# Stick-breaking attention: stay factors kept and scanned in PSUM, the mask as a matrix product

## The chip, the cores and the metric

One NeuronCore of a Trainium2 chip runs the whole kernel in one launch. The metric is the device time of that launch in microseconds; the core is the only one, so it is also the slowest. PE is the matrix engine, DVE the vector engine, ACT the activation engine, POOL GpSimd, SP the engine whose queue issues the DMAs. [...]

## The reference

One transformer layer on 2048 tokens of width 1024: adaptive layer norm, an input projection, three mixers (gated chunks, stick-breaking attention, dilated-window attention), an output projection, and a feed-forward part with a causal convolution. The change touches the stick-breaking mixer, six heads of width 64:

```python
z = jnp.einsum('bqhd,bkhd->bhqk', q_blk, k).astype(jnp.float32) * scale      # scale = 1/8
log_beta = jax.nn.log_sigmoid(z)
log_stay = jnp.where(before, jax.nn.log_sigmoid(-z), 0.0)                     # before: k_pos < q_pos
tail = lax.cumsum(log_stay, axis=3, reverse=True) - log_stay
weight = jnp.where(before, jnp.exp(log_beta + tail), 0.0)
return jnp.einsum('bhqk,bkhd->bqhd', weight.astype(v.dtype), v)
```

The weight of key k for query q is sigmoid(z) at k times the product of sigmoid(-z) over all keys between k and q. The kernel works with these products directly, without logarithms: it scans the stay factors sigmoid(-z) from the last key to the first with a running product.

## The kernel before

All matrix products are in fp32 precision by splitting each operand into a high and a low part (fp32r) and adding three products. Instructions are put in order on each engine by a planner that simulates the program on a cost model of its own; each engine then runs its own list strictly in that order and waits on semaphores. `ORDER` (L1152) lists the units of work for the two halves of the sequence (c = 0 and 1, 1024 tokens each). `st0` to `st5` are stick-breaking heads, `sx5` is head 5 of the first half done in the second list, and a unit with `~` runs aside: after each key chunk of a stick head a few of its steps are released, by the numbers of `RATE`. In the first half the heads lie among projections (`gmv`, `gm`), rotations (`rot`, `stage`) and loads; in the second half, after `rel` (L1090), the six heads run together with the output projection (`op`, `wo_hi`, `yraw`, `xo`) aside. `free` (L1096) gives the stick's memory back, and the FFN takes it for its weights.

`stick` (L498) treats one head for one half. A group g is 256 queries, two blocks j of 128. For each group it goes over key chunks kc of 512 keys, from the one that holds the diagonal (`diag`, kc = top) down to 0. In the diagonal chunk only `nb` blocks of 128 keys exist, so tiles are 128 to 512 wide. The first half has one or two key chunks per group, the second three or four. For each kc and j:

- PE: scores `z` in a PSUM bank, two products (L527, L528).
- ACT: `stay` = sigmoid(-z/8) into one of three long-lived SBUF tiles of 513 columns whose last column is 1.0 (L532), then `beta` = sigmoid(z/8) into SBUF (L533). The z bank is free after that.
- POOL, diagonal only: two `affine_select` on the last 128 columns, setting `stay` to 1 and `beta` to 0 where key >= query (L536).
- DVE: `tensor_tensor_scan` over `stay` backwards, 513 columns, both operands the same SBUF view, initial value 1.0 or the carry of the chunk before (L540), into a new `excl` tile of 513 columns (four slots). Because it starts in the column of ones, `excl` shifted by one is the exclusive product.
- POOL: `beta` times the shifted `excl` (helper `tt`, L78).
- PE: `nb` transposes into the PSUM tile `tr` (L546). ACT copies it to `wh` (helper `copy`, L70), DVE writes the low part `wl` = tr - wh (L78).

After both j, PE adds the products of `wh` and `wl` with the values into `av` (L557). PSUM has eight banks: up to `rel` three for `gm`, two for `z`, two for `tr`, one for `av`; after `rel` two for `gm`, two for `z`, three for `tr`, one for `av` (L1094, L1147).

The tag `excl` serves a second purpose at the start: `ada_first` (L162), called in four steps, takes its accumulator `ada_acc` and the raw V weights of each step from the same four slots. PE reads each accumulator in `ada_ps` (L177).

Of the kernel before, what the change touches and what calls it, by code (L numbers as in the profile page):

```python
# [5 lines left out]
F32 = mybir.dt.float32  # L6
F32R = mybir.dt.float32r
BF16 = mybir.dt.bfloat16
I32 = mybir.dt.int32
AF = mybir.ActivationFunctionType  # L10
ALU = mybir.AluOpType
# [32 lines left out]
class Kernel:  # L44
# [443 lines left out]


    def stick_const(self):  # L490
        self.stay = []
        for k in range(3):
            t = self.pa.tile([P, 513], F32, name=f"stay{k}")
            self.nc.gpsimd.memset(t, 1.0)
            self.stay.append(t)
        self.stay_i = 0

    def stick(self, h, c):  # L498
        nc = self.nc
# [7 lines left out]
        for g in range(4 * c, 4 * c + 4):  # L507
# [3 lines left out]
                av2 = self.ps.tile([P, 512], F32, name="av", tag="av")  # L511
            qo = (g % 2) * 256
            av = av2[:, qo:qo + 256]
            carry = [None, None]
            top = g // 2
            for kc in range(top, -1, -1):
                wh = self.pa.tile([P, 4, 256], F32R, name="wh", tag="wh")
                wl = self.pa.tile([P, 4, 256], F32R, name="wl", tag="wl")
                nbs = []
                for j in range(2):  # L520
                    diag = kc == top
                    nb = (2 * g + j) % 4 + 1 if diag else 4
                    nbs.append(nb)
                    n, o = nb * P, 512 - nb * P
                    kk = khat[kc // 2][:, (kc % 2) * 512:]
                    z = self.ps.tile([P, 512], F32, name="z", tag="z")
                    nc.tensor.matmul(z[:, :n], q1[:, qo + j * P:qo + (j + 1) * P], kk[:, :n], start=True, stop=False)  # L527
                    nc.tensor.matmul(z[:, :n], q2[:, qo + j * P:qo + (j + 1) * P], kk[:, :n], start=False, stop=True)  # L528
                    s = self.stay[self.stay_i]
                    self.stay_i = (self.stay_i + 1) % len(self.stay)  # L530
                    b = self.pa.tile([P, 512], F32, name="beta", tag="beta")
                    nc.scalar.activation(s[:, o:512], z[:, :n], AF.Sigmoid, scale=-0.125)  # L532
                    nc.scalar.activation(b[:, o:512], z[:, :n], AF.Sigmoid, scale=0.125)  # L533
                    if diag:
                        for t, fill in ((s, 1.0), (b, 0.0)):
                            nc.gpsimd.affine_select(out=t[:, 384:512], in_=t[:, 384:512], pattern=[[-1, P]],  # L536
                                                    compare_op=ALU.is_gt, fill=fill, base=0, channel_multiplier=1)
                    x = self.pa.tile([P, 513], F32, name="excl", tag="excl")
                    sr = s[:, o:513][:, ::-1]
                    nc.vector.tensor_tensor_scan(x[:, o:513][:, ::-1], sr, sr, 1.0 if diag else carry[j],  # L540
                                                 op0=ALU.mult, op1=ALU.bypass)
                    carry[j] = x[:, o:o + 1]
                    self.tt("beta", b[:, o:512], b[:, o:512], x[:, o + 1:513], ALU.mult)
                    tr = self.ps.tile([P, 4, P], F32, name="tr", tag="tr")
                    for e in range(nb):
                        nc.tensor.transpose(tr[:, e, :], b[:, o + e * P:o + (e + 1) * P], self.ident)  # L546
                    js = slice(j * P, (j + 1) * P)
                    self.copy("whi_s", wh[:, :nb, js], tr[:, :nb, :])
                    self.tt("v", wl[:, :nb, js], tr[:, :nb, :], wh[:, :nb, js].bitcast(F32), ALU.subtract)
                ops = [(0, 0, wh)]  # L550
                if nbs[1] > nbs[0]:
                    ops += [(nbs[0], P, wh), (nbs[0], P, wl)]
                for e in range(1, nbs[0]):
                    ops += [(e, 0, wh), (e, 0, wl)]
                ops.append((0, 0, wl))
                for m, (e, q0, w) in enumerate(ops):
                    last = nc.tensor.matmul(av[:, q0:256], vhat[kc // 2][:, (kc % 2) * 4 + e, :], w[:, e, q0:256],  # L557
                                            start=(kc == top and m == 0), stop=(kc == 0 and m == len(ops) - 1))
                yield last.ins, sum(nbs) / 8.0
# [287 lines left out]
    def run(self):  # L847
# [191 lines left out]
        for c, order in enumerate(ORDER):  # L1039
            u = units(c, hT[c])  # L1040
            for token in order.split():
# [48 lines left out]
                elif what == "rel":  # L1090
                    finish()
                    self.p1.release()
                    self.ps.release()
                    self.ps = _Bufs(self.pool("ps2", space=PSUM), {**BUFS, "gm": 2, "tr": 3})  # L1094
                    self.po = _Bufs(self.pool("po"), BUFS)
                elif what == "free":  # L1096
                    finish()
# [46 lines left out]

ENGINES = {"whi0": "a", "wlo0": "pppv", "lnt0": "a", "hlo0": "pppv", "lnt": "va", "lnx00": "avv", "lnx01": "aav", "lnx10": "v", "lnx11": "v", "lnx": "va", "hlo": "pvv", "whi": "v", "wlo": "pvv", "qkhi": "avv", "qklo": "v", "cqk": "a", "rot1": "ppv", "rot2": "pv", "rot3": "v", "rothi": "aav", "rotlo": "pvv", "sgu1": "pv", "sgu2": "p", "sguhi": "ap", "sgulo": "ppv", "ya": "aaav", "fold": "a", "beta": "p", "whi_s": "a", "whi_d": "avv", "wom": "v", "wohi": "aav", "wolo": "pv", "ysc": "pv", "yhi": "av", "ylo": "pv", "wuhi": "v", "wulo": "pvv", "wdm": "p", "wdhi": "av", "wdlo": "ppv", "upc": "av", "gv": "pppv", "ghi": "ap", "glo": "ppv", "vhi": "av", "vlo": "v", "uc": "v"}

BUFS = {"gm": 3, "z": 2, "tr": 2, "av": 1, "wraw": 2, "whi": 3, "wlo": 3, "s8": 3, "cs": 2, "tmp2": 2, "khat": 3, "vhat": 2, "q": 2, "beta": 4, "excl": 4, "wh": 2, "wl": 2, "fold": 1, "ys": 1, "x4": 2, "yraw": 2, "ysc": 4, "yh": 2, "yl": 2, "xo": 3, "wuraw": 4, "wul": 3, "wuh": 3, "wdraw": 2, "fx": 2, "up": 3, "dn": 5, "wdh": 2, "wdl": 2, "upc": 3, "cv": 3, "gh": 4, "gl": 4, "fs": 4, "fry": 2, "frr": 2}  # L1147

WOUT = 6
EARLY = (0, 1, 5, 6, 7)  # L1150
# [39 lines left out]
```

## Time and profile before

| what | value |
|---|---|
| median of 3 runs | 2831.44 us (2830.4 to 2834.19) |
| the profiled execution's own time | 2831.72 us |
| its span in the trace | 2830.0 us |
| PE busy | 2639.5 us, 93% |
| DVE busy | 2182.7 us, 77% |
| POOL busy | 1197.3 us, 42% |
| ACT busy | 987.6 us, 35% |
| stick-breaking scans, all | 144 carried (mean 1574 ns), 96 diagonal |

The busy shares are averages over the whole span; the program has stages with different limits, so the views below are read by stretch (us from the span's start). The rows in the section on the trace name an instruction by line of the kernel, engine, operation and tiles (written tile first, then the tiles read), its shape and its count. "Idle before" is time that the engine stood still just ahead of these instructions, with the instruction whose end released it. Matmuls overlap each other, so PE's busy time is not time at its peak.

### The profile page before, as it was taken

To read this page: it belongs to the slowest core of one execution; us is meant where nothing else is said; L and a number is where in the kernel's file an instruction comes from. 1 tells how busy PE (TensorE), PEld (TensorE's weight loads), DVE (VectorE), ACT (ScalarE), POOL (GpSimd) and SP (SyncE) were. 2 spreads that over 40 slices of the span, in tenths; PEclk is the share of its full clock that TensorE was granted. 3 is DMA by queue.
4 is the path that set the end of the run, shared out by engine and by line. 5 is a ranking of instruction groups with operands and counts; after the bars stand their busy time and mean duration, and the time that the engine had idled before them with its cause. 6 is when DMAs were issued, how large, how long until landed. Compare 5 with 4: busy or idle time off the path is not lost.

```text
span 2830.0 us, 37108 instructions
## 1 busy us (share of the span) xinstructions
PE 2639.5 (93%) x13334; PEld 2208.6 (78%) x13334; DVE 2182.7 (77%) x3188; ACT 987.6 (35%) x1841; POOL 1197.3 (42%) x1138
## 2 busy tenths in 40 slices
PE   7989899899887888899999999999998999999997
PEld 6868897788866777777788888888877888888886
DVE  5587888766589999964787777777888778777776
ACT  5244444333455666633222112122262212112113
POOL 3276524330158776722444333334444333433323
PEclk9989999999988999999999999999999999999999
DMA  7645485878564332258211111111133111111111
GB/s 233 198 114 164 140 292 173 225 186 215 141 179 127 93 93 66 79 180 297 67 55 50 52 46 45 45 45 53 47 117 119 45 45 60 45 53 45 45 38 60
DMA packets 305300, 309.40 MB, mean 109 GB/s; under 512 B 65516, under 2 KB 245596, under 8 KB 305116
## 3 DMA queue, kind: packets, MB, share of 16 engines
q1 hardware_dynamic: 305116, 307.02, 36.8%
q8 instruction: 106, 1.74, 0.3%
q14 instruction: 78, 0.64, 0.1%
HBM read 232.36 MB, written 68.30 MB: 106 GB/s over the span
## 4 chain that ended last, share of the span: by engine, by line
PE 62%; DVE 15%; DMA 9%; issue 6%; POOL 4%; ACT 3%; SPq 1%; DVEq 0%; POOLq 0%; ACTq 0%
PE up L93 11%; PE up L94 11%; PE up L92 11%; PE dn L94 5%; PE dn L92 5%; PE dn L93 5%; DVE excl L540 3%; PE gmv L342 2%; POOL beta L78 2%; DMA wraw<-in_w_in_dram 2%; PE av L557 2%; SPq L83 1%; DMA wada<-in_w_ada_dram 1%; DVE wl L78 1%; PE tr L546 1%
## 5 line engine op out<-in xcount | busy, mean ns | idle before, releaser
L92 PE MATMUL up<-gh,wuh 128*128 128x512 f32 x1408 | 552.8, 393 | 2.1 <-ACT gh L260 2.1
L94 PE MATMUL up<-gh,wul 128*128 128x512 f32 x1408 | 554.5, 394 | 0.0
L93 PE MATMUL up<-gl,wuh 128*128 128x512 f32 x1408 | 554.3, 394 | 0.0
L821 DVE TENSOR_TENSOR acc<-dn,acc 128x512 f32<-128x512 f32 x688 | 441.4, 681 | 104.3 <-PE dn L94 103.6
L779 DVE SCALAR_TENSOR_TENSOR cv<-upc,cw,cv 128x512 f32<-128x512 f32 x352 | 339.9, 966 | 104.1 <-ACT cv L777 101.0
L78 POOL TENSOR_TENSOR beta<-beta,excl 128x128 f32<-128x128 f32 (+2 forms) x240 | 310.8, 1308 | 140.7 <-DVE excl L540 101.1
L92 PEld LDWEIGHTS up<-gh,wuh 128*128 128x128 f32 x1408 | 264.7, 188 | 62.0 <-ACT gh L260 2.3
L93 PEld LDWEIGHTS up<-gl,wuh 128*128 128x128 f32 x1408 | 265.0, 188 | 61.2 <-issue 0.2
L94 PEld LDWEIGHTS up<-gh,wul 128*128 128x128 f32 x1408 | 264.8, 188 | 59.8 <-issue 0.2
L92 PE MATMUL dn<-wdh,gh 128*128 128x512 f32 x688 | 271.3, 395 | 11.6 <-DVE acc L821 10.4
L93 PE MATMUL dn<-wdl,gh 128*128 128x512 f32 x688 | 271.2, 394 | 0.0
L94 PE MATMUL dn<-wdh,gl 128*128 128x512 f32 x688 | 256.6, 396 | 0.0
L777 ACT ACTIVATE cv<-up,cb 128x512 f32<-128x512 f32 x176 | 136.6, 776 | 284.6 <-DVE upc L72 284.6
L540 DVE TENSOR_TENSOR_SCAN excl<-stay,excl 128x513 f32<-128x513 f32 x144 | 224.6, 1574 | 2.0 <-ACT stay L532 1.9
L70 ACT ACTIVATE upc<-up 128x512 f32<-128x512 f32 x88 | 52.5, 597 | 379.7 <-PE up L94 379.6
L70 ACT ACTIVATE wh<-tr 128x128 fp32r<-128x128 f32 (+2 forms) x240 | 128.5, 541 | 161.2 <-PE tr L546 150.4
L72 DVE CAST wuh<-wuraw 128x512 fp32r<-128x512 f32 x176 | 131.3, 785 | 63.5 <-PE up L93 58.3
L546 PE MATMUL tr<-ident,beta 128*128 128x128 f32 x816 | 139.4, 292 | 37.1 <-POOL beta L78 26.5
L342 PE MATMUL gmv<-wlo,hh 128*128 128x256 f32 x576 | 169.5, 295 | 2.5 <-DVE wlo L78 1.4
L774 POOL COPY upc<-upc 128x2 f32<-128x2 f32 x88 | 20.7, 235 | 353.6 <-DVE upc L72 302.2
L342 PE MATMUL gmv<-whi,hh 128*128 128x256 f32 x576 | 169.0, 294 | 1.3 <-DVE vst L78 1.3
L78 POOL TENSOR_TENSOR wlo<-wraw,whi 128x512 fp32r<-128x512 f32 x35 | 53.4, 1529 | 275.2 <-DVE whi L72 178.3
(249 smaller groups left out, 6092.5 us busy)
## 6 DMA issues: line engine op xcount, KB each, us to landing
wuraw<-in_w_up_dram SPq DMA_DIRECT2D x176, 256.0 KB, 3.2
wdraw<-in_w_down_dram SPq DMA_DIRECT2D x44, 512.0 KB, 3.5
wada<-in_w_ada_dram SPq DMA_DIRECT2D x32, 512.0 KB, 5.7
wraw<-in_w_in_dram SPq DMA_DIRECT2D x112, 128.0 KB, 4.7
vd<-vst SPq DMA_DIRECT2D x12, 1024.0 KB, 5.3
q<-bq SPq DMA_DIRECT2D x48, 256.0 KB, 4.3
q<-cq SPq DMA_DIRECT2D x48, 256.0 KB, 4.2
x<-xo SPq DMA_DIRECT2D x24, 512.0 KB, 6.0
```

The costliest lines, as they stand in the source:

```text
L70: self.nc.scalar.activation(out, in_, AF.Copy)
L72: self.nc.vector.tensor_copy(out, in_)
L78: (self.nc.vector if eng == "v" else self.nc.gpsimd).tensor_tensor(out=out, in0=a, in1=b, op=op)
L92: self.nc.tensor.matmul(ps, ah, bh, start=(k == 0), stop=False)
L93: self.nc.tensor.matmul(ps, ah, bl, start=False, stop=False)
L94: self.nc.tensor.matmul(ps, al, bh, start=False, stop=(k == n - 1))
L342: self.nc.tensor.matmul(ps[:, e, :], a[:, o:o + P], b, start=(n == 0), stop=(n == 3 * KB - 1))
L540: nc.vector.tensor_tensor_scan(x[:, o:513][:, ::-1], sr, sr, 1.0 if diag else carry[j], op0=ALU.mult, op1=ALU.bypass)
L546: nc.tensor.transpose(tr[:, e, :], b[:, o + e * P:o + (e + 1) * P], self.ident)
L777: nc.scalar.activation(t, ps, AF.Identity, bias=self.cb[:, blk:blk + 1], scale=self.cw[2][:, blk:blk + 1])
L779: nc.vector.scalar_tensor_tensor(out=t, in0=u[:, tap:tap + TG], scalar=self.cw[tap][:, blk:blk + 1], in1=t, op0=ALU.mult, op1=ALU.add)
L821: nc.vector.tensor_tensor(out=acc[t][:, ns], in0=ps, in1=acc[t][:, ns], op=ALU.add)
```

## The change

The stay factors are no longer written to SBUF. ACT writes `beta` first, then overwrites z in its PSUM bank with sigmoid(-z/8), and the scan reads z from there; its second operand, which the operation ignores, is `beta`. The column of ones goes: the scan covers n columns, not n + 1, and its result goes to one half of an `excl` tile of 1025 columns that a block j keeps for all its key chunks. The halves alternate with kc, so that the carry of the chunk before stands right behind the new half (right half first, then left); when the right half is written a second time, in the third key chunk, POOL copies the carry into the last column. The tile has three slots instead of four.

The two selects go. Instead a constant matrix `after` (-1e30 where key >= query, else 0) is added to the diagonal block of the scores by a product with the identity, between the two score products; the sigmoids then give stay 1 and beta 0. In the diagonal chunk the last key's product is left out on POOL (m = n - 1), since its weight is 0.

After `rel`, `z` has three PSUM banks and `tr` two; the constants are made by POOL in `stick_const`.

```diff
--- before.py
+++ after.py
@@ -488,12 +488,16 @@
 
 
     def stick_const(self):
-        self.stay = []
-        for k in range(3):
-            t = self.pa.tile([P, 513], F32, name=f"stay{k}")
-            self.nc.gpsimd.memset(t, 1.0)
-            self.stay.append(t)
-        self.stay_i = 0
+
+        nc = self.nc
+        self.ident_r = self.pa.tile([P, P], F32R, name="ident_r")
+        nc.gpsimd.tensor_copy(self.ident_r, self.ident)
+        self.after = self.pa.tile([P, P], F32R, name="after")
+        t = self.pa.tile([P, P], F32, name="after_t", tag="fold")
+        nc.gpsimd.memset(t, 0.0)
+        nc.gpsimd.affine_select(out=t, in_=t, pattern=[[-1, P]], compare_op=ALU.is_gt, fill=NEG, base=0,
+                                channel_multiplier=1)
+        nc.gpsimd.tensor_copy(self.after, t)
 
     def stick(self, h, c):
         nc = self.nc
@@ -511,39 +515,43 @@
                 av2 = self.ps.tile([P, 512], F32, name="av", tag="av")
             qo = (g % 2) * 256
             av = av2[:, qo:qo + 256]
-            carry = [None, None]
             top = g // 2
+            excl = [None, None]
             for kc in range(top, -1, -1):
                 wh = self.pa.tile([P, 4, 256], F32R, name="wh", tag="wh")
                 wl = self.pa.tile([P, 4, 256], F32R, name="wl", tag="wl")
                 nbs = []
+                diag = kc == top
+
+                x0 = 512 if (top - kc) % 2 == 0 else 0
                 for j in range(2):
-                    diag = kc == top
                     nb = (2 * g + j) % 4 + 1 if diag else 4
                     nbs.append(nb)
-                    n, o = nb * P, 512 - nb * P
+                    n = nb * P
                     kk = khat[kc // 2][:, (kc % 2) * 512:]
+                    qs = slice(qo + j * P, qo + (j + 1) * P)
                     z = self.ps.tile([P, 512], F32, name="z", tag="z")
-                    nc.tensor.matmul(z[:, :n], q1[:, qo + j * P:qo + (j + 1) * P], kk[:, :n], start=True, stop=False)
-                    nc.tensor.matmul(z[:, :n], q2[:, qo + j * P:qo + (j + 1) * P], kk[:, :n], start=False, stop=True)
-                    s = self.stay[self.stay_i]
-                    self.stay_i = (self.stay_i + 1) % len(self.stay)
+                    nc.tensor.matmul(z[:, :n], q1[:, qs], kk[:, :n], start=True, stop=False)
+                    if diag:
+                        nc.tensor.matmul(z[:, n - P:n], self.ident_r, self.after, start=False, stop=False)
+                    nc.tensor.matmul(z[:, :n], q2[:, qs], kk[:, :n], start=False, stop=True)
                     b = self.pa.tile([P, 512], F32, name="beta", tag="beta")
-                    nc.scalar.activation(s[:, o:512], z[:, :n], AF.Sigmoid, scale=-0.125)
-                    nc.scalar.activation(b[:, o:512], z[:, :n], AF.Sigmoid, scale=0.125)
+                    nc.scalar.activation(b[:, :n], z[:, :n], AF.Sigmoid, scale=0.125)
+                    nc.scalar.activation(z[:, :n], z[:, :n], AF.Sigmoid, scale=-0.125)
                     if diag:
-                        for t, fill in ((s, 1.0), (b, 0.0)):
-                            nc.gpsimd.affine_select(out=t[:, 384:512], in_=t[:, 384:512], pattern=[[-1, P]],
-                                                    compare_op=ALU.is_gt, fill=fill, base=0, channel_multiplier=1)
-                    x = self.pa.tile([P, 513], F32, name="excl", tag="excl")
-                    sr = s[:, o:513][:, ::-1]
-                    nc.vector.tensor_tensor_scan(x[:, o:513][:, ::-1], sr, sr, 1.0 if diag else carry[j],
+                        excl[j] = self.pa.tile([P, 1025], F32, name="excl", tag="excl")
+                    x = excl[j]
+                    before = 1.0 if diag else x[:, 512 - x0:513 - x0]
+                    nc.vector.tensor_tensor_scan(x[:, x0:x0 + n][:, ::-1], z[:, :n][:, ::-1], b[:, :n][:, ::-1], before,
                                                  op0=ALU.mult, op1=ALU.bypass)
-                    carry[j] = x[:, o:o + 1]
-                    self.tt("beta", b[:, o:512], b[:, o:512], x[:, o + 1:513], ALU.mult)
+                    if not diag and x0:
+                        nc.gpsimd.tensor_copy(x[:, 1024:1025], before)
+
+                    m = n - 1 if diag else n
+                    self.tt("beta", b[:, :m], b[:, :m], x[:, x0 + 1:x0 + 1 + m], ALU.mult)
                     tr = self.ps.tile([P, 4, P], F32, name="tr", tag="tr")
                     for e in range(nb):
-                        nc.tensor.transpose(tr[:, e, :], b[:, o + e * P:o + (e + 1) * P], self.ident)
+                        nc.tensor.transpose(tr[:, e, :], b[:, e * P:(e + 1) * P], self.ident)
                     js = slice(j * P, (j + 1) * P)
                     self.copy("whi_s", wh[:, :nb, js], tr[:, :nb, :])
                     self.tt("v", wl[:, :nb, js], tr[:, :nb, :], wh[:, :nb, js].bitcast(F32), ALU.subtract)
@@ -1091,7 +1099,7 @@
                     finish()
                     self.p1.release()
                     self.ps.release()
-                    self.ps = _Bufs(self.pool("ps2", space=PSUM), {**BUFS, "gm": 2, "tr": 3})
+                    self.ps = _Bufs(self.pool("ps2", space=PSUM), {**BUFS, "gm": 2, "z": 3})
                     self.po = _Bufs(self.pool("po"), BUFS)
                 elif what == "free":
                     finish()
@@ -1144,7 +1152,7 @@
 
 ENGINES = {"whi0": "a", "wlo0": "pppv", "lnt0": "a", "hlo0": "pppv", "lnt": "va", "lnx00": "avv", "lnx01": "aav", "lnx10": "v", "lnx11": "v", "lnx": "va", "hlo": "pvv", "whi": "v", "wlo": "pvv", "qkhi": "avv", "qklo": "v", "cqk": "a", "rot1": "ppv", "rot2": "pv", "rot3": "v", "rothi": "aav", "rotlo": "pvv", "sgu1": "pv", "sgu2": "p", "sguhi": "ap", "sgulo": "ppv", "ya": "aaav", "fold": "a", "beta": "p", "whi_s": "a", "whi_d": "avv", "wom": "v", "wohi": "aav", "wolo": "pv", "ysc": "pv", "yhi": "av", "ylo": "pv", "wuhi": "v", "wulo": "pvv", "wdm": "p", "wdhi": "av", "wdlo": "ppv", "upc": "av", "gv": "pppv", "ghi": "ap", "glo": "ppv", "vhi": "av", "vlo": "v", "uc": "v"}
 
-BUFS = {"gm": 3, "z": 2, "tr": 2, "av": 1, "wraw": 2, "whi": 3, "wlo": 3, "s8": 3, "cs": 2, "tmp2": 2, "khat": 3, "vhat": 2, "q": 2, "beta": 4, "excl": 4, "wh": 2, "wl": 2, "fold": 1, "ys": 1, "x4": 2, "yraw": 2, "ysc": 4, "yh": 2, "yl": 2, "xo": 3, "wuraw": 4, "wul": 3, "wuh": 3, "wdraw": 2, "fx": 2, "up": 3, "dn": 5, "wdh": 2, "wdl": 2, "upc": 3, "cv": 3, "gh": 4, "gl": 4, "fs": 4, "fry": 2, "frr": 2}
+BUFS = {"gm": 3, "z": 2, "tr": 2, "av": 1, "wraw": 2, "whi": 3, "wlo": 3, "s8": 3, "cs": 2, "tmp2": 2, "khat": 3, "vhat": 2, "q": 2, "beta": 4, "excl": 3, "wh": 2, "wl": 2, "fold": 1, "ys": 1, "x4": 2, "yraw": 2, "ysc": 4, "yh": 2, "yl": 2, "xo": 3, "wuraw": 4, "wul": 3, "wuh": 3, "wdraw": 2, "fx": 2, "up": 3, "dn": 5, "wdh": 2, "wdl": 2, "upc": 3, "cv": 3, "gh": 4, "gl": 4, "fs": 4, "fry": 2, "frr": 2}
 
 WOUT = 6
 EARLY = (0, 1, 5, 6, 7)
```

## Rows read from the trace of the kernel before

**Rows 1.** Busy time by stretch: length, engines (instructions), granted clock, DMA.
```profile
core 0: us, PE busy (x) PEld busy (x) DVE busy (x) ACT busy (x) POOL busy (x), PEclk, DMA share, GB/s
...
200.00:300.00 100.00, 88.18 (x597) 82.02 (x598) 82.99 (x92) 40.55 (x81) 68.15 (x63) 0.95 0.54 154
...
1300.00:2830.00 1530.00, 1498.47 (x6515) 1218.25 (x6513) 1181.92 (x1687) 373.28 (x584) 582.52 (x544) 0.99 0.20 63
...
820.00:1215.00 395.00, 332.46 (x1886) 273.33 (x1887) 367.74 (x384) 246.81 (x506) 296.77 (x273) 0.93 0.36 99
```

**Rows 2.** Chain of waits in 820 to 1215 us; two pieces: start, length, what.
```profile
by line: DVE excl L540 17.0%; issue 13.6%; POOL beta L78 11.5%; PE av L557 8.0%; DVE wl L78 5.9%; PE tr L546 5.4%; PE op L101 3.9%; PE op L102 3.7%; PE op L100 3.4%; POOL stay L536 2.4%; DMA vhat<-vd 2.3%; DMA ycraw<-yc 2.2%; ACT stay L532 
...
1169.49 1.11 POOL beta L78
1170.59 0.77 issue
```

**Rows 3.** DVE groups, 820 to 1215 us: count | busy, mean ns | idle before, releasers.
```profile
L540 DVE TENSOR_TENSOR_SCAN excl<-stay,excl 128x513 f32<-128x513 f32 x116 | 183.3, 1595 | 0.2 <-ACT stay L532 0.2
L78 DVE TENSOR_TENSOR wl<-tr,wh 128x512 fp32r<-128x512 f32 x129 | 84.3, 669 | 9.5 <-ACT wh L70 9.5
L540 DVE TENSOR_TENSOR_SCAN excl<-stay 128x513 f32<-128x513 f32 x12 | 17.3, 1442 | 3.8 <-POOL stay L536 3.6
...
L540 DVE TENSOR_TENSOR_SCAN excl<-stay 128x385 f32<-128x385 f32 x12 | 12.7, 1057 | 4.2 <-POOL stay L536 3.6
...
L540 DVE TENSOR_TENSOR_SCAN excl<-stay 128x257 f32<-128x257 f32 x11 | 10.0, 909 | 4.8 <-POOL stay L536 4.5
...
L540 DVE TENSOR_TENSOR_SCAN excl<-stay 128x129 f32<-128x129 f32 x11 | 6.8, 617 | 3.3 <-POOL stay L536 2.9
```

**Rows 4.** In order of time, DVE, then POOL: start us, us, what, count, [idle before].
```profile
1155.05 1.28 DVE L540 TENSOR_TENSOR_SCAN excl<-stay,excl 128x513 f32<-128x513 f32 x1
...
1156.83 1.84 DVE L540 TENSOR_TENSOR_SCAN excl<-stay,excl 128x513 f32<-128x513 f32 x1
...
1169.26 3.23 DVE L540 TENSOR_TENSOR_SCAN excl<-stay,excl 128x513 f32<-128x513 f32 x2
...
1156.50 1.09 POOL L78 TENSOR_TENSOR beta<-beta,excl 128x512 f32<-128x512 f32 x1 [1.36 <-DVE excl L540]
...
1169.49 8.88 POOL L78 TENSOR_TENSOR beta<-beta,excl 128x512 f32<-128x512 f32 x5 [2.03 <-DVE excl L540]
```

**Rows 5.** Three tiles on DVE: duration ns min/median/max, first and last start, forms.
```profile
L78 DVE TENSOR_TENSOR wl<-tr,wh x163: 259/660/693, 819.7 to 1212.8; 128x512 fp32r<-128x512 f32 x129, 128x384 fp32r<-128x384 f32 x12, 128x128 fp32r<-128x128 f32 x11, 128x256 fp32r<-128x256 f32 x11
...
L736 DVE TENSOR_TENSOR xo<-op,xo x48: 656/680/692, 906.5 to 1320.8; 128x512 f32<-128x512 f32 x48
...
L78 DVE TENSOR_TENSOR wlo<-wraw,whi x53: 658/681/2260, 31.4 to 775.5; 128x512 fp32r<-128x512 f32 x53
```

**Rows 6.** POOL groups, 820 to 1215 us.
```profile
L78 POOL TENSOR_TENSOR beta<-beta,excl 128x512 f32<-128x512 f32 x129 | 186.2, 1456 | 77.8 <-DVE excl L540 46.9 <-PE tr L546 6.9 <-ACT beta L533 6.7
L536 POOL TENSOR_SCALAR_AFFINE_SELECT stay<-stay 128x128 f32<-128x128 f32 x46 | 24.3, 529 | 3.6 <-PE z L528 2.8 <-ACT stay L532 0.8
```

**Rows 7.** ACT and PE groups, 850 to 1210 us.
```profile
L532 ACT ACTIVATE stay<-z 128x512 f32<-128x512 f32 x118 | 71.4, 605 | 33.2 <-PE z L528 29.5 <-DVE excl L540 2.7 <-PE av L557 0.3
...
L546 PE MATMUL tr<-ident,beta 128*128 128x128 f32 x543 | 89.8, 286 | 27.0 <-POOL beta L78 22.9 <-DVE wl L78 3.6
...
L527 PE MATMUL z<-khat,q 128*128 128x512 f32 x118 | 53.3, 451 | 0.0
```

**Rows 8.** DVE and POOL groups, 100 to 620 us.
```profile
L540 DVE TENSOR_TENSOR_SCAN excl<-stay,excl 128x513 f32<-128x513 f32 x24 | 34.8, 1460 | 1.8 <-ACT stay L532 1.8
...
L536 POOL TENSOR_SCALAR_AFFINE_SELECT stay<-stay 128x128 f32<-128x128 f32 x48 | 29.6, 617 | 22.2 <-ACT stay L532 22.2
```

**Rows 9.** In order of time at the start, SP's queue and PE.
```profile
32.53 2.46 SPq L83 DMA_DIRECT2D wraw<-in_w_in_dram  x5
...
35.92 0.28 PE L177 MATMUL ada_ps<-ones,ada_acc 128*128 128x1 f32 x2
```


## The prediction

> **What bounds the kernel now.** I read the busy times by stretch first [rows 1]. Stick-breaking runs in two places. A chunk is one query block j against one key chunk kc. The 72 chunks of the first 1024 tokens lie scattered between 100 and 620 us among projections, rotations and loads. Of the 168 of the second 1024 tokens, 162 stand together from 820 to 1215 us, with the output projection as filler. In that stretch DVE is busy 367.7 of 395 us (93%), PE 332.5, POOL 296.8, ACT 246.8. After 1215 us the FFN has PE busy 98%, no scan in it, and its weight loads need the memory that the stick's pool gives back: the second stretch's end passes on to the end of the program one for one.
>
> Second view: the chain of waits inside 820 to 1215 [rows 2]. It goes through the scan (17.0%), "issue" (13.6%, 54 us), POOL's product beta (11.5%) and POOL's select on `stay` (2.4%), DVE and POOL by turns. The reader should look at one "issue" piece: 0.77 us between two POOL products that wait for no semaphore.
>
> Third: what DVE does there [rows 3]. 128 full scans (116 with a carried value, 12 diagonal) take 183.3 + 17.3 = 200.6 us, the three narrower widths 29.5 us, 129 full wl subtractions 84.3 us. DVE's idle 27.3 us is named in the same rows: 14.6 us behind the select on `stay` (3.6 + 3.6 + 4.5 + 2.9), 9.5 us behind ACT's wh, the rest small.
>
> Fourth: the same instructions in order of time [rows 4]. A carried scan takes 1.28 us at 1155.05, with no POOL product until 1156.50, and 1.84 us at 1156.83, when POOL began a product 0.33 us earlier. From 1169.3 two scans take 3.23 us and five POOL products 8.88 us, though one product alone takes 1.09. So a scan and a POOL instruction do not run together: the later one waits, counted as its busy time or as "issue". The scan reads two operands in SBUF. wl, which reads one from PSUM and one from SBUF, is not stretched beside the same POOL: 163 of them, median 660, longest 693 ns [rows 5]. This is what the prediction rests on.
>
> **The change, part by part.**
> *The scan's source.* Its first operand moves to PSUM (z), the second (bypassed) is b in SBUF: the operand places of wl, not of the old scan. I take 1.28 us for a full one, as alone. From below: 512 for 513 elements, no gain worth counting. From above: the 1.60 mean of today [rows 3], if nothing is relieved. Does PSUM as source cost? A 512-wide product out of PSUM (xo) has median 680 ns, one with both operands in SBUF (wlo) 681 [rows 5]: nothing. Saved: 200.6 - 128 x 1.28 = 36.8 us; the narrower widths by the same ratio (1.28/1.58 = 0.81), 29.5 x 0.19 = 5.6 us. Together 42.4 us of DVE.
> [...]
>
> *The mask by a matrix product.* Both selects of a diagonal chunk go from POOL (0.53 us each on `stay` [rows 6]), and with them DVE's 14.6 us. In their place comes a 128-column PE product in each of the 46 diagonal chunks of the stretch; bounded by a transpose of as many columns (286 ns [rows 7]) that is at most 13.2 us on PE, and at least nothing, since matmuls overlap. DVE's length hides it: 332.5 + 13.2 = 345.7 us. It has no more cover than that, so PE is what comes next.
>
> *Order on ACT.* b comes first and the scan waits for both sigmoids: 0.605 us later [rows 7]. In mid-head DVE is behind and does not notice; at the start of each of the 24 groups it can, where it waited for the selects until now. I take 10 of the possible 24 x 0.605 = 14.5 us as new idle time (below: 0).
>
> *The carry copy.* 48 one-column POOL copies, each under the 0.53 us of a select: at most 25 us on a POOL that loses 92 selects, and issued while the scan runs, with the product behind it waiting for that scan anyway. Cost 0. *Excl halves.* A scan into the right half overwrites an element that the product two chunks earlier reads; a scan and a wl stand between (1.95 us against 1.09): 0.
>
> *PSUM slots.* z stays occupied until the scan has read it. With three slots in the second stretch: two products of at most 0.45, two sigmoids 1.21, scan 1.28 and hand-offs, about 3.7 us, so 1.2 us per chunk against the 2.0 that DVE needs (325.3/162, below): 0. tr falls from three to two; see the rivals.
>
> Sum for the stretch: 367.7 - 42.4 = 325.3 us of DVE work, 12.7 us of idle time that stays, 10 new: 348, for 395. **Gain 47 us**; without new idle time 57.
>
> *The first half.* The 24 carried scans at 1.45 would fall by 34.8 - 24 x 1.28 = 4.1 us, and POOL loses 96 selects, 29.6 us for those on `stay` alone [rows 8]. But DVE is 83% and PE 88% busy there [rows 1] and loads and rotations stand in the chain too. z keeps two slots, now held through the scan, and 48 mask products come to PE. I take a gain of 4 us, between 15 gained and 67 lost (rival three).
>
> *The start.* excl has three slots, not four, and the first loads use them: the third step's V weight would take the slot of the second step's accumulator, which PE's last product for that step leaves at 36.2 us, while that load is the last of five issued from 32.53 on SP [rows 9]. Behind it on SP stand the last step's w_ada loads. About 1 us, between 0 and 2.
>
> Sum, from the profiled execution (2831.72 us for a span of 2830.0; the median of the runs is 0.28 lower, which I ignore): 2831.7 - 47 - 4 + 1 = **2782 us**. Own range 2768 to 2797.
>
> **Rivals.**
> 1. *The transposed tile takes over.* With two tr slots, each is held through 4 transposes (about 0.6 us), wh (as long as a sigmoid, 0.6), wl (0.67) and, where DVE runs two scans between, 2.56 us; with hand-offs 4.6 us, so 2.3 us per chunk, above DVE's 2.0. Then 162 x 2.3 = 373 us: gain 22 + 3, 2807 us. For it: the trace has scans in pairs (3.23 us x2 [rows 4]). Against: one scan between would make 1.66 us per chunk.
> 2. *The scan still blocks POOL*, because its second operand comes from SBUF. Only the selects go: -14.6, +10 for ACT, and the selects (24.3 us on `stay` alone [rows 6]) no longer contend with scans, say 6: 2821 us. Against: wl has the same places and its longest is 693 ns.
> 3. *Slower: PE is held in the first half.* PE takes instructions in order; a z product whose slot is still under a scan stops all projections behind it. The hold grows by 0.6 + 1.28 us; over two slots 0.94 us per chunk, 72 x 0.94 = 67 us: 2832 - 47 + 67 = 2852 us. It decides from 51/72 = 0.7 us per chunk. For it: other DVE work can stand ahead of a scan there. Against: the chunks are sparse, 72 in 520 us, 7.2 us each, where two slots can turn one in about 1.85 (3.7/2).
>
> **Chances.** Forecast 0.60; rival 1 0.20; rival 2 0.06; rival 3 0.10; everything cancels 0.04 (within 0.2%, 2826 to 2837, about what a measurement here can tell from none). Faster 0.86, same 0.04, slower 0.10. For 8 in 10 the range runs from 2764 (no new idle time and 7 us more in the first half) to 2818.
>
> **What will show it.** In the second stretch: full scans at a mean of 1.27 to 1.33 us with a longest below 1.6; POOL's full products at about 1.1, not 1.46; "issue" down from 13.6% of the chain; no select; DVE still the busiest, wl and xo unchanged; length near 348 us. I am wrong if the scans stay near 1.6 (rival 2), if PE's transposes wait for wl and DVE idles for wh (rival 1), or if the stretch before 820 us grows (rival 3). The FFN after it should keep its length.

## The result: 37 us faster, and what the profile after shows

Four runs of the changed kernel have a median of 2793.6 us (2788.9 to 2798.0), four of the kernel before beside them 2830.9 (2827.2 to 2834.2). The ratio is 0.9868 with a 95% interval of [0.9845, 0.9892]: faster by 1.3%. 2782 was forecast, with a range of 2764 to 2818. The profiled execution of the change is the slowest of its four (2798.0), so the parts below add up to a gain of 33.7 us and not of 37.

Four events cut the span into parts: PE's first gate product, just before the second half of the stick-breaking; the first load of an FFN weight (`wuraw`), which needs the memory that the stick gives back; the first FFN product; the end. The groups of three tiles give them (count, ns min/median/max, first and last start in us). Before:

```profile
L224 PE MATMUL gate_ps<-gacc,ones x8: 592/592/697, 823.1 to 1348.4; 128*128 128x512 f32 x8
...
L83 SPq DMA_DIRECT2D wuraw<-in_w_up_dram x176: 367/368/1629, 1238.3 to 2736.2; - x176
...
L92 PE MATMUL up<-gh,wuh x1408: 387/392/628, 1322.7 to 2792.7; 128*128 128x512 f32 x176
```

After:

```profile
L224 PE MATMUL gate_ps<-gacc,ones x8: 592/826/1220, 821.5 to 1315.1; 128*128 128x512 f32 x8
...
L83 SPq DMA_DIRECT2D wuraw<-in_w_up_dram x176: 367/368/1279, 1200.3 to 2703.6; - x176
...
L92 PE MATMUL up<-gh,wuh x1408: 387/392/628, 1289.4 to 2760.0; 128*128 128x512 f32 x176
```

| part of the span, us | before | after | difference |
|---|---|---|---|
| start to the gate product | 823.1 | 821.5 | -1.6 |
| gate product to the `wuraw` load (called the second half below) | 415.2 | 378.8 | -36.4 |
| `wuraw` load to the first FFN product | 84.4 | 89.1 | +4.7 |
| first FFN product to the end | 1507.3 | 1506.9 | -0.4 |
| span of the profiled executions | 2830.0 | 2796.3 | -33.7 |

So the gain is the second half. The last part did not change; the third lies anywhere between 83 and 90 us in the kernels below, whatever their second half.

The granted clock of the second half rose too, from 0.93 to 0.96. Before, after, and run 2 below (columns as in [rows 1]):

```profile
823.10:1238.30 415.20, 353.45 (x1983) 290.62 (x1984) 374.24 (x395) 246.33 (x504) 298.13 (x271) 0.93 0.36 99
...
821.50:1200.30 378.80, 349.09 (x2018) 289.94 (x2019) 327.26 (x393) 242.83 (x505) 211.69 (x227) 0.96 0.39 108
...
825.40:1239.30 413.90, 348.62 (x1987) 285.88 (x1988) 377.00 (x395) 246.60 (x505) 296.13 (x271) 0.96 0.35 98
```

The clock is not the cause of the gain: run 2 has 0.96 as well, and its second half is as long as before.

The stretch that answers to 820 to 1215 us [rows 1] is 815 to 1181. Busy time (instructions) of PE, its weight loads, DVE, ACT and POOL, then granted clock and DMA:

```profile
815.00:1181.00 366.00, 332.95 (x1937) 275.60 (x1937) 323.65 (x386) 243.54 (x508) 211.81 (x228) 0.96 0.38 108
```

It is 29 us shorter and holds one chunk more (163). The other 7 us of the second half lie outside it: it begins 6.5 us ahead of the gate product instead of 3.1, and ends 19.3 us ahead of the `wuraw` load instead of 23.3. DVE lost 44 us of work, POOL 85; PE kept its 333 and is now the busiest (91% of 366 us), where the prediction's signs had DVE. Where DVE's time went, by its groups there (count | busy us, mean ns | idle before, releasers), as in [rows 3]:

```profile
L545 DVE TENSOR_TENSOR_SCAN excl<-z,excl,beta 128x512 f32<-128x512 f32 x117 | 149.4, 1277 | 11.4 <-ACT z L540 9.2 <-issue 0.3
L78 DVE TENSOR_TENSOR wl<-tr,wh 128x512 fp32r<-128x512 f32 x129 | 87.1, 675 | 22.9 <-ACT wh L70 22.9
L545 DVE TENSOR_TENSOR_SCAN excl<-z,beta 128x512 f32<-128x512 f32 x12 | 14.6, 1216 | 1.8 <-ACT z L540 1.8
...
L545 DVE TENSOR_TENSOR_SCAN excl<-z,beta 128x384 f32<-128x384 f32 x12 | 11.3, 944 | 0.0
...
L545 DVE TENSOR_TENSOR_SCAN excl<-z,beta 128x256 f32<-128x256 f32 x11 | 7.6, 689 | 0.0
...
L545 DVE TENSOR_TENSOR_SCAN excl<-z,beta 128x128 f32<-128x128 f32 x11 | 4.6, 415 | 0.0
```

The carried scan fell from 1595 to 1277 ns; `wl` kept its length. In order of time, DVE and then POOL, as in [rows 4] (start us, us, what, idle before):

```profile
1100.42 1.27 DVE L545 TENSOR_TENSOR_SCAN excl<-z,excl,beta 128x512 f32<-128x512 f32 x1
...
1102.20 1.27 DVE L545 TENSOR_TENSOR_SCAN excl<-z,excl,beta 128x512 f32<-128x512 f32 x1
...
1110.90 1.19 DVE L78 TENSOR_TENSOR yl<-yraw,yh 128x1024 fp32r<-128x1024 f32 x1
...
1101.84 1.10 POOL L78 TENSOR_TENSOR beta<-beta,excl 128x512 f32<-128x512 f32 x1 [0.65 <-DVE excl L545]
...
1111.13 1.92 POOL L78 TENSOR_TENSOR beta<-beta,excl 128x512 f32<-128x512 f32 x1 [2.48 <-DVE excl L545]
```

POOL's product at 1101.84 and the scan that starts at 1102.20 overlap, and neither is stretched. At 1111.13 the product takes 1.92 us: DVE is in `yl`, whose two operands are both in SBUF. POOL's groups, which answer to [rows 6]:

```profile
L78 POOL TENSOR_TENSOR beta<-beta,excl 128x512 f32<-128x512 f32 x118 | 136.6, 1158 | 115.9 <-DVE excl L545 100.8 <-PE tr L554 11.6 <-PE op L102 2.9
...
L548 POOL COPY excl<-excl 128x1 f32<-128x1 f32 x46 | 12.5, 271 | 0.0
```

The chain of waits in the stretch, to hold against [rows 2]: `beta` and the select on `stay` have left its head.

```profile
by line: DVE excl L545 20.2%; PE av L565 10.5%; issue 8.7%; DVE wl L78 7.0%; PE tr L554 6.6%; ACT beta L539 4.9%; ACT z L540 4.3%; PE op L101 4.1%; PE op L102 4.1%; PE op L100 4.0%; DMA vhat<-vd 3.4%; PE z L534 3.0%; ACT wh L70 2.6%; PE z L
```

And the waits of DVE, then of PE's weight loads, over the stretch (us in total, times, longest):

```profile
DVE wl L78 <- ACT wh L70: 22.9, 36, 2.2
DVE excl L545 <- ACT z L540: 11.0, 35, 0.6
DVE gate L225 <- DMA yraw<-yT: 4.0, 1, 4.0
...
PEld av L565 <- DVE wl L78: 19.3, 23, 2.8
PEld z L534 <- DVE excl L545: 18.1, 34, 1.7
```

The last line is new: PE waits for a slot of z that a scan still reads.

### The profile page after: what moved, and what is told of

Same layout as the page of the kernel before. It is cut to its first block, busy times and chain, and to the rows that moved or that the text cites. A ratio compares the mean times of both kernels' runs of the same rounds, so it can differ in the third digit from the quotient of the medians.

```text
span 2796.3 us, 36851 instructions
## 1 busy us (share of the span) xinstructions
PE 2641.1 (94%) x13430; PEld 2210.9 (79%) x13430; DVE 2122.0 (76%) x3188; ACT 983.0 (35%) x1842; POOL 1043.6 (37%) x995
## 4 chain that ended last, share of the span: by engine, by line
PE 61%; DVE 13%; DMA 9%; ACT 4%; issue 3%; POOL 1%; SPq 1%; DVEq 0%; POOLq 0%; ACTq 0%
PE up L93 11%; PE up L94 11%; PE up L92 11%; PE dn L94 5%; PE dn L92 5%; PE dn L93 5%; DVE excl L545 3%; PE gmv L342 3%; DMA wada<-in_w_ada_dram 2%; PE av L565 2%; DMA wraw<-in_w_in_dram 1%; DVE wl L78 1%; SPq L83 1%; PE tr L554 1%; PE op L102 1%
## 5 line engine op out<-in xcount | busy, mean ns | idle before, releaser
L78 POOL TENSOR_TENSOR beta<-beta,excl 128x127 f32<-128x127 f32 (+2 forms) x240 | 258.4, 1080 | 290.6 <-DVE excl L545 259.9
L545 DVE TENSOR_TENSOR_SCAN excl<-z,excl,beta 128x512 f32<-128x512 f32 x144 | 183.7, 1276 | 19.5 <-ACT z L540 17.1
L78 DVE TENSOR_TENSOR wl<-tr,wh 128x128 fp32r<-128x128 f32 (+2 forms) x240 | 141.3, 594 | 39.7 <-ACT wh L70 39.6
L342 PE MATMUL gmv<-whi,hl 128*128 128x256 f32 x576 | 169.5, 296 | 1.0 <-DVE hl L78 0.9
L92 PEld LDWEIGHTS dn<-wdh,gh 128*128 128x128 f32 x688 | 129.9, 189 | 43.1 <-DVE acc L829 11.9
```

Of the source, the lines that this page charges most:

```text
L78: (self.nc.vector if eng == "v" else self.nc.gpsimd).tensor_tensor(out=out, in0=a, in1=b, op=op)
L92: self.nc.tensor.matmul(ps, ah, bh, start=(k == 0), stop=False)
L342: self.nc.tensor.matmul(ps[:, e, :], a[:, o:o + P], b, start=(n == 0), stop=(n == 3 * KB - 1))
L545: nc.vector.tensor_tensor_scan(x[:, x0:x0 + n][:, ::-1], z[:, :n][:, ::-1], b[:, :n][:, ::-1], before, op0=ALU.mult, op1=ALU.bypass)
```

## The experiments

The change has several edits in one. The theory was the prediction's: a scan with two operands in SBUF and a POOL instruction shut each other out (1.28 us for a scan alone, 1.84 beside a POOL product [rows 4]), and moving one operand to PSUM ends that. Its rivals: the gain is that of the selects; or that of scanning in place. Ratios are against runs of the kernel before on the same chip, with 95% intervals; the runs come from more than one chip, on which the kernel before has medians of 2829.4 to 2830.9 us. "Gate" and "second half" are the events above, of one profiled execution each.

| kernel | us | ratio | gate | second half |
|---|---|---|---|---|
| before | 2830.9 | 1 | 823.1 | 415.2 |
| the change | 2793.6 | 0.9868 [0.9845, 0.9892] | 821.5 | 378.8 |
| 1 second operand in PSUM, nothing else | 2794.6 | 0.9869 [0.9849, 0.9890] | 813.2 | 391.0 |
| 2 the same, an SBUF column | 2833.8 | 1.0013 [1.0002, 1.0023] | 825.4 | 413.9 |
| 3 mask product alone | 2845.4 | 1.0052 [1.0039, 1.0066] | 853.7 | 401.0 |
| 4 the change, selects back | 2809.2 | 0.9928 [0.9914, 0.9942] | 823.4 | 393.6 |
| 5 the change, three tr slots, two z | 2803.9 | 0.9907 [0.9893, 0.9921] | 828.5 | 380.0 |
| 6 operand and mask product | 2801.1 | 0.9894 [0.9879, 0.9909] | 833.0 | 376.4 |
| 7 mask product in the second half | 2808.8 | 0.9924 [0.9912, 0.9937] | 821.1 | 394.0 |
| 8 the change, less PE work (one run) | 2782.3 | | 815.9 | 368.8 |
| 9 the change, less DVE work (one run) | 2781.6 | | 825.5 | 359.9 |
| 10 operand, mask product in the second half | 2783.3 | 0.9829 [0.9814, 0.9844] | 808.5 | 380.4 |
| 11 like 10, work moved from DVE to POOL | 2785.5 | 0.9844 [0.9831, 0.9858] | 807.5 | 378.0 |
| 12 operand, mask product in the first half (one run) | 2799.3 | | 827.9 | 380.8 |

**1. One operand.** The kernel before; the scan's second operand, which `op1=bypass` ignores, becomes one column of z in PSUM, repeated n + 1 times. Stay factors, selects and tiles remain.

```
-  tensor_tensor_scan(x[:, o:513][:, ::-1], sr, sr, ...
+  tensor_tensor_scan(x[:, o:513][:, ::-1], sr, z[:, 0:1].broadcast_to([P, n + 1]), ...
```

> The kernel before with one edit: the scan's second, ignored operand is a PSUM column of z read over and over instead of the SBUF view of stay. Selects, widths, banks and slots stay as they were; z is now held until the scan. Theory A (the gain comes from a scan with two SBUF operands no longer excluding POOL): full scans between 820 and 1215 us fall from a mean of 1.595 to about 1.28 us with a longest under 1.4, POOL's full products from 1.46 to about 1.1, the selects from 0.53 to about 0.3; total 2795 to 2812 us. Theory B (the gain comes from taking the selects off the diagonal path): no change, 2827 to 2835. Theory C (scanning out of PSUM is itself quicker): no change either, since stay is still read from SBUF.

This edit alone gives the whole change's time, with the selects kept and the stay factors still in SBUF, though in other parts: in its profile 9.9 us come ahead of the gate product and 24.2 in the second half, where the change has 1.6 and 36.4. The groups of `excl` and `stay` (ns min/median/max):

```profile
L540 DVE TENSOR_TENSOR_SCAN excl<-stay,excl,z x144: 1245/1270/1285, 140.0 to 1178.9; 128x513 f32<-128x513 f32 x144
...
L536 POOL TENSOR_SCALAR_AFFINE_SELECT stay<-stay x96: 285/295/1534, 118.6 to 1165.7; 128x128 f32<-128x128 f32 x96
```

The longest of 144 carried scans is 1285 ns. Over 810 to 1184 us POOL's products and its selects on `stay` fall too, from 1456 and 529 ns [rows 6]:

```profile
L78 POOL TENSOR_TENSOR beta<-beta,excl 128x512 f32<-128x512 f32 x131 | 148.8, 1138 | 113.6 <-DVE excl L540 104.1 <-PE tr L546 3.0 <-PE op L102 2.8
L536 POOL TENSOR_SCALAR_AFFINE_SELECT stay<-stay 128x128 f32<-128x128 f32 x46 | 17.3, 377 | 5.7 <-ACT stay L532 5.6
```

And DVE waits 4.1 us for the selects instead of 14.6 [rows 3]:

```profile
DVE excl L540 <- ACT beta L533: 18.8, 32, 2.8
DVE wl L78 <- ACT wh L70: 18.4, 23, 3.3
...
DVE excl L540 <- POOL stay L536: 4.1, 9, 1.1
```

**2. The control.** The same edit with a column of b, in SBUF.

```
+  tensor_tensor_scan(x[:, o:513][:, ::-1], sr, b[:, o:o + 1].broadcast_to([P, n + 1]), ...
```

> The control to the second-operand run: the kernel before, and the scan's ignored operand is again one column read over and over, but a column of beta in SBUF instead of one of z in PSUM. If the place of the operand is what counts (theory A): scans stay stretched, mean 1.5 to 1.6 us in the second half, total 2826 to 2840 us. If the repeated column as such is quicker, or the longer hold of z changes the order for the better: about 2795 us, as with the PSUM column.

```profile
L540 DVE TENSOR_TENSOR_SCAN excl<-stay,excl,beta x144: 1250/1507/3410, 142.2 to 1213.3; 128x513 f32<-128x513 f32 x144
```

No gain. That the operand repeats one column, is another tile than the first, or makes the scan wait for one sigmoid more is therefore not it; its place is. In run 1, with the column in PSUM, the longest carried scan took 1285 ns; here, with it in SBUF, 3410. Why the place counts, the runs don't show.

**3. The mask alone.** The kernel before; both selects go, the matrix product comes. For it identity and mask are also held as float32r constants, made at the start.

```
+  if diag:
+      nc.tensor.matmul(z[:, n - P:n], self.ident_r, self.mask_r[:, P + 1:2 * P + 1], start=False, stop=False)
...
-  if diag:
-      for t, fill in ((s, 1.0), (b, 0.0)):
-          nc.gpsimd.affine_select(...)
```

> The kernel before with only the mask by a matrix product: the two selects go, the scan still reads stay from SBUF with both operands. Theory A: the scans keep a mean of 1.5 to 1.6 us, DVE's 14.6 us behind the selects go; total 2815 to 2825 us. Theory B: most of the gain is here, 2790 to 2803 us. Theory C: as A, 2815 to 2825.

Slower by 0.5%, which no theory had (2815 to 2825, or 2790 to 2803), in two parts with opposite signs: the second half falls by 14.2 us, the gate product comes 30.6 us later. The carried scans from 850 to 1234 us stay long:

```profile
L544 DVE TENSOR_TENSOR_SCAN excl<-stay,excl 128x513 f32<-128x513 f32 x116 | 178.7, 1556 | 2.0 <-ACT stay L540 1.2 <-POOL beta L78 0.5
```

**4. The change without its mask product.** The selects are back, and the stay factors of a diagonal chunk go to the unused half of `excl`, in SBUF, where POOL selects on them.

```
-  if diag: nc.tensor.matmul(z[:, n - P:n], self.ident_r, self.after, ...)
+  s = x[:, 0:512] if diag else z
+  nc.scalar.activation(s[:, :n], z[:, :n], AF.Sigmoid, scale=-0.125)
+  if diag: for t, fill in ((s, 1.0), (b, 0.0)): nc.gpsimd.affine_select(...)
```

> The changed kernel with the selects put back: the diagonal chunk's stay factors are written to the unused half of excl in SBUF and masked there by POOL; all other chunks are scanned in PSUM. Theory A: the carried scans stay at 1.28 us, DVE waits again 10 to 18 us for selects; total 2800 to 2812 us. Theory B: the gain is gone, 2825 to 2835. If the parts add up, the gain of this one and of the mask alone together make the 37 us of the whole change.

15.6 us slower than the change, 14.8 of it in the second half. It holds both kinds of scan in one run, from PSUM and b, and from `excl` and b, and only the second kind is stretched (median 1016 ns, longest 3154; the same four widths have 812 and 1224 in run 1):

```profile
L548 DVE TENSOR_TENSOR_SCAN excl<-z,excl,beta x144: 1247/1272/1306, 140.2 to 1192.9; 128x512 f32<-128x512 f32 x144
L548 DVE TENSOR_TENSOR_SCAN excl<-excl,beta x96: 407/1016/3154, 120.8 to 1180.4; 128x128 f32<-128x128 f32 x24, 128x256 f32<-128x256 f32 x24, 128x384 f32<-128x384 f32 x24, 128x512 f32<-128x512 f32 x24
```

**5. Slots.** `{"gm": 2, "z": 3}` of the second stretch becomes `{"gm": 2, "tr": 3}`, with z at two: a test of rival 1, which moves two counts at once.

> The changed kernel with the PSUM banks of the kernel before in the second half: z two, tr three. What kept the stretch at 366 us and not 348? If the two tr slots do (rival 1 of the prediction): DVE's 22.9 us behind wh fall to about 10 and the total to 2780 to 2788 us. If it is PE's own order and load: no gain. If three z slots are needed: PE's waits for z behind the scan grow from 28 us to over 50, ACT and DVE starve, and the total rises to 2798 to 2815 us.

DVE waits less for wh and more for z, over 816 to 1182 us, and the second half is no shorter (380.0):

```profile
DVE excl L545 <- ACT z L540: 21.0, 44, 2.5
DVE wl L78 <- ACT wh L70: 10.2, 15, 3.4
```

So a third tr slot paid for with a z slot gains nothing; what it is worth beside three z slots wasn't tried. The total came out 10 us longer, in the third range of the expectation, and PE's weight loads wait longer for z, as it said (34.8 us for 18.1). But the second half is only 1.2 us longer; 7.0 lie ahead of the gate product (828.5, not 821.5), where nothing was changed: up to some 11 us ahead of that product the two traces have the same instructions on PE in the same order. So 7 us are what this event scatters by itself.

**6 and 7. Do the edits add up?** Run 6 is runs 1 and 3 together; run 7 is run 3 with the product where `c == 1` (second half) and the selects where `c == 0`.

> Both parts on the kernel before, without scanning in place: second operand from PSUM and mask by a matrix product, stay still in SBUF, banks z two and tr three. The second half (first gate product to first w_up load: 415 us before, 391 with the operand alone, 401 with the mask alone) should add up to about 377 us. If the 30 us that the mask alone lost before 820 us come from the mask itself, the total is 2805 to 2815 us; if they come from the order of that one program or from the scans that still excluded POOL, it is 2776 to 2788 us.

> The mask by a matrix product in the second half only; the first half keeps POOL's selects; the constants are made at the same place as with the mask alone. If the mask in the first half loses the 30 us there: first gate product at about 823 us and a total of 2814 to 2822 us. If making the constants early does: about 850 us and 2840 to 2850 us, as with the mask alone.

In the second half they do, as far as single profiles can tell (see runs 10 to 12): 415.2 - 24.2 (run 1) - 14.2 (run 3) = 376.8, run 6 has 376.4 and the change 378.8. No gain of scanning in place shows there. Both totals missed: run 6 lies between its two ranges, run 7 below its lower one. In the first half the mask product costs: with it the gate product stands at 853.7 (run 3), without it at 821.1 (run 7), though the constants are made at the start in both.

**8 and 9. What bounds the second half now.** Run 8 takes most of the `wl` products from PE (168 of 432 stay), run 9 the subtraction for `wl` from DVE (`wl = wh`, so that PE's products remain). Both leave out the weights' low part, run 8 some of it and run 9 all.

```
-  ops += [(e, 0, wh), (e, 0, wl)]
+  ops += [(e, 0, wh)]            # run 8
...
-  self.tt("v", wl[:, :nb, js], tr[:, :nb, :], wh[:, :nb, js].bitcast(F32), ALU.subtract)
+  wl = wh                        # run 9
```

> The changed kernel without the products of the low parts wl of all key blocks but one or two of a chunk (part of the weights' low half is left out): PE loses about 3 of 8 value products of a full chunk pair, some 70 us of recorded busy time, DVE and POOL nothing. If PE is what the second half (378.8 us from first gate product to first w_up load) now waits for: 350 to 360 us. If DVE is: 372 to 380 us.

> The changed kernel without the subtraction that makes wl (wh is used in its place, so the low part is left out): DVE loses 163 subtractions, some 100 us, and the wait for wh; PE does the same. If DVE bounds the second half: it goes to PE's load, 335 to 350 us. If PE does: 370 to 380 us.

The second half of run 8, then of run 9, to hold against the change's row above:

```profile
815.90:1184.70 368.80, 326.39 (x1816) 262.35 (x1817) 329.80 (x394) 242.93 (x505) 210.05 (x227) 0.97 0.40 109
...
825.50:1185.40 359.90, 332.85 (x2013) 285.19 (x2014) 238.06 (x229) 243.41 (x505) 207.93 (x227) 0.97 0.42 113
```

Run 8 has 202 PE products and 22.7 us of PE's busy time less, and is 10.0 us shorter; run 9 has 89.2 us of DVE's busy time less and is 18.9 us shorter. Each is one execution, and 10.0 us is no more than such profiles scatter, so only run 9's share is clear; but both totals lie below all four of the change's. Both second halves fall between the ranges expected for PE and for DVE as the bound: as far as these two show, neither engine sets it alone. In run 9, 816 to 1182 us, DVE waits for z although PE has as many products to do as in the change:

```profile
DVE excl L545 <- ACT z L540: 75.9, 79, 6.3
```

**10 to 12. The best of the parts.** Run 10 is run 1 with the mask product where `c == 1` alone; run 11 gives POOL two kinds of DVE products besides (`"wom": "p", "ysc": "p"`); run 12 is run 1 with the mask product where `c == 0` alone.

> The two parts that paid, each where it paid: second operand from PSUM everywhere, the mask by a matrix product in the second half only, selects in the first. From the marks: first gate product at 813 us as with the operand alone, then 376 us as with both: total 2776 to 2784 us, below both kernels. If the loss of the runs with the mask before 820 us comes from the constants or the planner's order and not from the mask in the first half: 2790 to 2803 us.

> As the run before, and the output projection's products with the gate and the scales (wom, ysc) all on POOL: DVE loses some 21 us in the second half and POOL, idle over 40% there, takes them. If DVE still takes part in the bound: the second half falls by 4 to 10 us, total 2768 to 2778 us. If PE and the hand-overs bound it, or POOL's long products delay beta behind them: 2778 to 2790 us.

> The mirror image: operand from PSUM everywhere, mask by a matrix product in the first half only. If the mask in the first half costs the time there: first gate product at 828 us or later, and the second half at about 391 us. If it was the planner's order by chance: 810 to 822 us.

Run 10 beats both kernels: its runs (2775.7 to 2784.8) all lie below the change's, and its ratio's interval just clears the change's. Its events:

```profile
L83 SPq DMA_DIRECT2D wuraw<-in_w_up_dram x176: 367/368/2895, 1188.9 to 2689.0; - x176
...
L229 PE MATMUL gate_ps<-gacc,ones x8: 592/592/697, 808.5 to 1302.1; 128*128 128x512 f32 x8
```

Its profiled span is 14.7 us shorter than the change's: 13.0 come from the first half, the second is 1.6 longer, the rest lies after it. Run 11 came out in its upper range: it cuts DVE's work from 328 of 368 us (803 to 1171) to 307 of 365 (803 to 1168) and the time doesn't move. Either DVE's work no longer sets it, or what POOL got (202 to 223 us) takes the gain back; the run doesn't tell the two apart. Run 12 again has a late gate product (827.9 against run 1's 813.2), but missed in the second half: 380.8, where the same code gave 391.0 in run 1. PE's order differs between the two from the gate product on, and from the first to the last scan they are 5.3 us apart (375.0 and 369.7). So one profile's second half can't be trusted to better than about 10 us, and the mask's worth there is only bounded: 4.4 (12 to 6), 10.6 (1 to 10), 14.2, 14.6 (1 to 6), 14.8, 21.2 us (before to 7).

## Why the prediction was right, and where its size was off

**The scan's source: right.** A full scan was put at 1.28 us and measured 1.277. Full scans of the stretch fell from 200.6 to 149.4 + 14.6 = 164.0 us, 36.6 against 36.8; the narrower from 29.5 to 11.3 + 7.6 + 11 x 0.415 = 23.5, 6.0 against 5.6. DVE's work came to 323.7 us for 325.3. Runs 1 and 2 show that the operand's place does it.

**PSUM costs the scan nothing: right.** The carried scans after, of the whole kernel (ns min/median/max):

```profile
L545 DVE TENSOR_TENSOR_SCAN excl<-z,excl,beta x144: 1249/1276/1291, 143.0 to 1177.6; 128x512 f32<-128x512 f32 x144
```

The shortest has 1249 ns, and 1250 in run 2 with both operands in SBUF. What is missing from the gain is idle time of DVE (42.3 us measured, 22.7 forecast), not longer scans.

**The selects: of the right size, as far as shown.** 14.6 us were put on them; runs 3 and 4 say 14.2 and 14.8, but the bounds above go from 4.4 to 21.2, and run 4 also scans its diagonal chunks from two SBUF operands. And they weren't needed for the gain: as POOL is freed by the scan, DVE's waits for them fall to 4.1 us by themselves (run 1).

**Order on ACT: the size right, the place wrong.** ACT's z makes DVE wait 11.0 us (10 forecast). But the prediction put this at the start of a group, in the diagonal chunk, and DVE behind in mid-head; 9.2 us stand ahead of the carried scans and 1.8 ahead of the full diagonal ones. That the number fits is luck.

**Carry copy, mask product: right.** 46 copies take 12.5 us of POOL (at most 25), and the mask product, from PE's groups of the stretch, 10.7 (at most 13.2):

```profile
L536 PE MATMUL z<-after,ident_r 128*128 128x128 f32 x45 | 10.7, 238 | 0.0
```

**The mis-sized term: the idle time that stays.** 12.7 + 10 = 22.7 us were forecast for DVE, 366 - 323.7 = 42.3 measured; with 1.6 less work that makes 366 instead of 348. The prediction carried the old 9.5 us behind wh over unchanged; it became 22.9. 4.0 more are one wait for a transfer ahead of the gate. The prediction's own sentence was that PE's work, at most 345.7 us (332.95 measured), comes next: two engines of nearly equal length that hand each chunk to each other through two or three slots, and the sum let the longer run at its full rate. Run 9 shows that such a loop doesn't: with 332.85 us of PE's busy time and 238.06 of DVE's it still took 359.9.

**PSUM slots: cost 0 was wrong in kind.** PE's weight loads wait 18.1 us for z slots held by scans (before: none for a scan). What this is worth alone wasn't tried: run 5 traded a z slot against a tr slot.

**First half: right within its bounds, by luck, the reason open.** -3 (-4 and +1 for the start) forecast, -1.6 measured. But with the operand alone the gate product stands at 813.2, 808.5 and 807.5 (runs 1, 10 and 11), 10 to 16 us ahead of before: that edit is worth more there than the 4 us forecast, and the change and run 5, at 821.5 and 828.5, give 8 us or more of it back. The wait of rival 3 is not what takes them: PE's weight loads wait less for z slots there in the change than in run 1, not more (100 to 808 us, the change, then run 1):

```profile
PEld z L534 <- DVE excl L545: 8.8, 12, 2.2
...
PEld z L527 <- DVE excl L540: 16.4, 19, 2.1
```

A first-half mask product with the stay factors in SBUF costs 14.7 (1 to 12), 24.5 (10 to 6) and 32.6 us (7 to 3). In place it can't be told apart: run 4, without the product, stands at 823.4, but scans its diagonal chunks from two SBUF operands. The constants aren't the cause, since runs 7 and 10 have them too. Whether it is the product on PE or the order of work that follows from it stays open. Scanning in place may spare the first half some of what run 6 paid (833.0 against 821.5 and 828.5); with 7 us of scatter that isn't shown.

**Rivals 1 and 2:** of the first's two signs one came: DVE idles 22.9 us for wh. The other didn't: PE's transposes hardly wait for wl (PE's waits, 815 to 1181 us):

```profile
PE tr L554 <- DVE wl L78: 0.7, 2, 0.4
```

So tr's slots don't hold PE, and run 5 gained nothing by a third tr slot. The length alone wouldn't have said so: 366 us are nearer to that rival's 373 than to the forecast's 348. Of the second nothing is left, with a longest scan of 1291 ns after, and "issue" at 8.7% of the chain instead of 13.6%.

**From the stretch to the time.** "One for one" nearly held: of 36.4 us, 4.7 were given back before the FFN and 1.6 came ahead.

## What to carry to other kernels

An operand that the operation ignores still counts by its place (2794.6 us with it in PSUM, 2833.8 in SBUF): where DVE and POOL work side by side, look for DVE instructions with both operands in SBUF and try one in PSUM, if only a column (here it was tried on the scan alone). The sign in a trace is a wide spread of durations for one shape (1250 to 3410 ns in run 2) and "issue" without a releaser (13.6% of the chain before, 8.7% after). When a bound engine is cut down to the next one's length, add up the waits anew: here 324 us of DVE and 333 of PE, feeding each other, took 366. And of a change in several edits, run each by itself: here one line gave all of it, and two of the edits, one of them in half the kernel only, were 10 us faster than all together.

## What was not expected of the hardware

POOL is held up as well as DVE, even in an instruction with one SBUF input: the selects on `stay` went from 529 to 377 ns, and the 512-wide product from 1456 to 1138 ns (run 1, 810 to 1184 us), when only the scan's ignored operand moved. A diagonal scan's time follows its length once it is free: 415, 689, 944 and 1216 ns for 128, 256, 384 and 512 elements, about 2.1 ns for each more, and some 60 more with a carried value (1277).
